# A far product weighted one tick later, and two merged first loads, in a hybrid attention and state-space trunk

## The chip, the cores and the metric

The kernel runs on one core of one Trainium2 chip. The metric is the device time of one execution in microseconds (us), the median of three runs. The core has five engines that work side by side: TensorE (PE in the profile, with its weight loads as PEld), VectorE (DVE), ScalarE (ACT), GpSimd (POOL) and SyncE (SP), and sixteen DMA engines that move data between the large memory and the core.

## The reference, cut to what matters

Two layers on 256 tokens of width 2048, each a mixer and an MLP, all in float32. Layer 0 mixes with latent attention (MLA), layer 1 with a Mamba-2 scan (SSM).

```python
def reference(x, ...):
    for i in range(DEPTH):                       # DEPTH = 2
        h = rms_norm(x, mix_norm_g[i])
        mix = mla_mixer(h, ...) if i % 2 == 0 else ssm_mixer(h, ...)
        x = x + mix
        h = rms_norm(x, mlp_norm_g[i])
        x = x + squared_relu_mlp(h, mlp_w_in[i], mlp_w_out[i])
    return x

# inside the scan of ssm_mixer, 8 groups g of 8 heads h of 64 channels p:
cb = einsum('blgn,bsgn->blsg', c_c, b_c)
y_diag = einsum('blsgh,bsghp->blghp', cb[..., None] * decay, x_c)
```

`y_diag` of the second 128 tokens gets one part from the first 128 tokens. That part is the far product: the inputs, weighted by their decay to the border of the halves, times `cb`, and then weighted by the decay from the border on.

## The kernel before, in words

**Matrix products.** Every weight is split into two rounded halves: ScalarE makes `wh` (line 102), VectorE makes `wl` = weight minus `wh` (line 103). A unit is two slices of 128 rows by 512 columns of a weight, 512 KB, loaded by SyncE into a tile `wraw` (line 85). TensorE runs over a unit 12 products of 128x512: eight with `wh` (lines 340 and 341, four of each), then four with `wl` (line 344). Loads and splits run some units ahead of TensorE; buffers of `wraw`, `wh` and `wl` come free as TensorE and the splits are done with them.

**The order of work.** TensorE's order is that of the program. Other engines get theirs from a scheduler when the kernel is built, and then run their rows strictly in that order. Side work is hung into the stream of products by `later(n, fn)`: `tick()` is called once per weight block of two units, and `fn` is run in the tick after n more ticks have passed.

**The start.** `start()` loads the first two units in two pieces of 512 columns each; after each piece, `some_x()` loads one piece of the transposed input `xT` (tiles named k). Then whole units and pieces of x alternate. `split_x` makes the halves `xt` of x on ScalarE (line 483) and VectorE (line 484). Unit 0 needs slices 0 and 1 of the first x tile, unit 1 slices 2 and 3, units 2 and 3 the second x tile.

**The SSM.** For each group g, `ahead()` lets GpSimd weight x (line 1393); two ticks later `across()` makes the far product on TensorE (line 1397) into a PSUM bank of the pool `sm` and VectorE weights it by `edge` into the tile `far` (line 1399). GpSimd adds `far` to the second half of x (line 1459) long after. The pool `sm` has two banks, handed out in program order; a product into a bank waits until all that was read from its earlier contents has been read. Other users of `sm` are the transposes of the convolution of B and C (line 1222), the products B times C (lines 1309 and 1310, read by line 1313) and the transposes of the finished output (line 323).

Of the kernel before, what the change touches and what calls it, by code (L numbers as in the profile page):

```python
# [24 lines left out]
ALU = mybir.AluOpType  # L25
# [190 lines left out]
class Trunk:  # L216
# [224 lines left out]
    def start(self, seq):  # L441
        nc, d = self.nc, self.d
        self.flow = Flow(nc, self.wp, seq, (6, 3))
        self.flow.tc = self.tc
        cst = self.c.tile([P, C_END], F32, name="cst")
        self.cst = cst
        self.ident_r = self.c.tile([P, P], F32R, name="ident")
        self.ident = self.ident_r.bitcast(F32)
        self.mhalf = self.c.tile([P, 16], F32, name="mhalf")
        warm = self.s2.tile([P, 512], F32R, tag="s2", name="warm")  # L450
        nc.vector.memset(warm.bitcast(F32), 1.0)
        bank = self.sm.tile([P, 512], F32, tag="sm", name="warmed")
        for _ in range(WARM):
            nc.tensor.matmul(bank, warm[:, :P], warm, start=True, stop=True)
        nc.gpsimd.memset(self.mhalf, -0.5)
        nc.scalar.dma_start(cst[:, C_G0:C_GQ], d["cst"][:, C_G0:C_GQ])
        nc.scalar.activation(self.stat(1), self.mhalf[:, :1], AF.Copy)
        raws = [self.ktile(self.k4, F32) for _ in range(4)]
        parts = [(0, slice(k, k + 1)) for k in range(4)] + [(1, slice(0, 2)), (1, slice(2, 4)), (2, slice(0, 4)), (3, slice(0, 4))]

        def some_x():
            j, k = parts.pop(0)
            nc.sync.dma_start(raws[j][:, k], d["xT"][j][:, k])

        self.flow.load(2, ((0, 512), (512, 1024)), some_x)
        for u in range(3, 7):
            some_x()
            self.flow.load(u)
        self.pos = self.c.tile([P, 2], I32, name="pos")
        self.x = [[self.res.tile([P, 512], F32, name=f"x{t}{n}") for n in range(4)] for t in range(2)]  # L470

        self.rs_pool = [self.c.tile([P, 4], F32, name=f"rs{i}") for i in range(2)]
        self.phase = 0
        self.xT = [(self.ktile(self.xtp), self.ktile(self.xtp)) for _ in range(4)]

        def split_x(j, ks):
            h, lo = self.xT[j]
            for k in ks:
                g = cst[:, C_G0 + 4 * j + k:C_G0 + 4 * j + k + 1]
                if (j, k) == (0, 0):  # L480
                    nc.vector.tensor_scalar(h[:, k], raws[j][:, k], g, None, ALU.mult)
                else:
                    nc.scalar.activation(h[:, k], raws[j][:, k], AF.Copy, scale=g)
                nc.vector.scalar_tensor_tensor(lo[:, k], raws[j][:, k], g, h[:, k].bitcast(F32), ALU.mult, ALU.subtract)

        split_x(0, (0,))
        self.flow.convert(1)
        split_x(0, (1, 2))
        self.flow.convert(2)
        split_x(0, (3,))  # L490
        self.flow.load(7)
        one = self.scratch()
        nc.sync.dma_start(one[:, :P], d["one"])
        nc.gpsimd.tensor_copy(self.ident_r, one[:, :P])
        nc.sync.dma_start(cst[:, C_GQ:], d["cst"][:, C_GQ:])
        nc.sync.dma_start(self.pos, d["pos"])
        split_x(1, range(4))
        ssq = self.stat(8)
        self.later(0, lambda: split_x(2, range(4)))
        self.later(1, lambda: split_x(3, range(4)))  # L500

        def stats(n):
            for t in range(2):
                nc.sync.dma_start(self.x[t][n], d["x"][t * P:(t + 1) * P, n * 512:(n + 1) * 512])
                self.square_sum(self.x[t][n], ssq[:, t * 4 + n:t * 4 + n + 1])
            if n == 3:
                self.set_rstd(ssq)

        for n, at in enumerate(X_AT):
            self.later(at, lambda n=n: stats(n))  # L510
# [666 lines left out]
    def ssm_body(self, sp, dp, gain, later):  # L1177
        nc, d, cst = self.nc, self.d, self.cst
# [8 lines left out]
        edge = sp.tile([P, 2, 64], F32, name="edge")  # L1187
# [6 lines left out]
        far = [None] * GROUPS  # L1194
# [17 lines left out]
        def behind(what):  # L1212
            return self.tc.issue_after(getattr(self.flow, what).ins)
# [108 lines left out]
        def x_rows(g, t0, n, first=3):  # L1322
            v = xD[0:P, g * 512:g * 512 + 512]
            row = v.ap[0][0]
            return bass.AP(tensor=v.tensor, offset=v.offset + (t0 * P + first) * row, ap=[[row, P], [P * row, n], [1, 512]])
# [11 lines left out]
        def x_conv(g, wait):  # L1337
            cw, tap, xts = {}, {}, []

            def weight(k):  # L1340
                cw[k] = sp.tile([P, 512], F32, tag="cw", name=f"cw{g}_{k}", bufs=3)
                nc.sync.dma_start(cw[k], d["cwx"][g][:, k * 512:(k + 1) * 512])

            def load(k):
                tap[k] = self.flow.pools["rx"].tile([P, 2, 512], F32, tag="rx", name=f"tap{g}_{k}")
                nc.sync.dma_start(tap[k], x_rows(g, 0, 2, k))

            def fetch(*todo):
                with behind("last_load"):
                    for fn in todo:  # L1350
                        fn()

            def whole():
                xts.append(xn.tile([P, 2, 512], F32, tag="xn", name=f"xtm{g}"))
                nc.sync.dma_start(xts[0], x_rows(g, 0, 2))

            both = lambda k: cw[k].unsqueeze(1).to_broadcast([P, 2, 512])
            plus = lambda v: nc.vector.tensor_tensor(xts[0], xts[0], v, ALU.add)

            def tapped(k):  # L1360
                nc.vector.tensor_tensor(tap[k], tap[k], both(k), ALU.mult)
                plus(tap[k])

            def mult():
                with behind("last_lo"):
                    nc.vector.tensor_tensor(xts[0], xts[0], both(3), ALU.mult)
                    tapped(2)
                fetch(lambda: weight(0), lambda: weight(4))

            def some():  # L1370
                with behind("last_lo"):
                    tapped(1)

            def total():
                with behind("last_lo"):
                    plus(both(4))
                    tapped(0)

            def tanh():
                tap[3] = self.flow.pools["rx"].tile([P, 2, 512], F32, tag="rx", name=f"th{g}")  # L1380
                with behind("last"):
                    nc.scalar.activation(tap[3], xts[0], AF.Tanh, scale=0.5)

            def silu():
                with behind("last_lo"):
                    nc.vector.scalar_tensor_tensor(xts[0], tap[3], 1.0, xts[0], ALU.add, ALU.mult)

            def ahead():
                x = xg[g] = [xts[0][:, t] for t in range(2)]
                heads_of = lambda v: v.rearrange("p (h f) -> p h f", h=8)  # L1390
                spread = lambda v: v[:, 8 * g:8 * g + 8].unsqueeze(2).to_broadcast([P, 8, 64])
                xw = self.scratch()
                nc.gpsimd.tensor_tensor(heads_of(xw), heads_of(x[0]), spread(edge[:, 0]), ALU.mult)

                def across():
                    b = self.bank(False)
                    nc.tensor.matmul(b, cb[g][:, P:256], xw, start=True, stop=True)
                    far[g] = sp2[0].tile([P, 512], F32, tag="far", name=f"far{g}", bufs=2)
                    nc.vector.tensor_tensor(heads_of(far[g]), heads_of(b), spread(edge[:, 1]), ALU.mult)

                self.later(2, across)

            self.later(wait, lambda: fetch(whole, lambda: weight(3), lambda: load(2), lambda: weight(2), lambda: load(1)))
            self.later(wait + 1, lambda: fetch(lambda: weight(1), lambda: load(0)))
            self.later(wait + 3, mult)
            self.later(wait + 4, some)
            self.later(wait + 4, lambda: cb_group(g))
            self.later(wait + 5, lambda: (total(), hq.extend((g, i) for i in range(8))))
            self.later(wait + 6, tanh)
            self.later(wait + 7, lambda: (silu(), ahead()))  # L1410
# [399 lines left out]
```

## Time and profile before

| | |
|---|---|
| median of 3 runs | 2279.67 us (2278.27 to 2280.44) |
| the profiled execution | 2280.21 us |
| its span, first to last instruction | 2278.4 us |
| TensorE busy | 2268.2 us, 100% |
| VectorE busy | 1967.8 us, 86% |
| ScalarE busy | 1438.9 us, 63% |
| GpSimd busy | 287.2 us, 13% |
| granted TensorE clock | 1.00 |

The time is the span and 1.8 us around it. TensorE is busy almost always, so that the places to look at are the few in which it waits.

### The profile page before, as it was taken

How to read it: one execution, taken by the hardware profiler on the slowest of the kernel's cores; microseconds unless marked ns; L12 is line 12 of the kernel's file. 1: busy time of each engine (PE TensorE's matmuls, PEld its weight loads, DVE VectorE, ACT ScalarE, POOL GpSimd, SP SyncE). 2: the span in 40 equal slices, each digit the busy share in tenths (PEclk: the TensorE clock that was granted, in tenths of full speed). 3: DMA queues.
4: the chain of work that ended last, by engine and by line, in shares of the span. 5: the costliest groups of instructions: out<-in, count | busy, mean ns of one | idle time of the engine just before them, and what ended most of it. 6: DMA issues, size and time to landing. Idle time of an engine off the chain costs nothing.

```text
span 2278.4 us, 30861 instructions
## 1 busy us (share of the span) xinstructions
PE 2268.2 (100%) x10881; PEld 1880.6 (83%) x10881; DVE 1967.8 (86%) x2257; ACT 1438.9 (63%) x2044; POOL 287.2 (13%) x339
## 2 busy tenths in 40 slices
PE   9999999999999999999999999999999999999999
PEld 7898888888888888888888788888888888888887
DVE  7786697998998898879989998976989989989995
ACT  7775475566666566566677676564665665665663
POOL 1440000000000000100002532230000000000000
PEclk9999999999999999999999999999999999999999
DMA  8545688888888887768898889877788888888874
GB/s 316 173 153 155 218 226 263 260 261 260 263 255 261 269 242 239 236 199 256 275 365 287 291 292 328 274 224 224 218 253 251 258 268 245 266 279 239 263 237 160
DMA packets 176026, 569.74 MB, mean 250 GB/s; under 512 B 20192, under 2 KB 29344, under 8 KB 175872
## 3 DMA queue, kind: packets, MB, share of 16 engines
q1 hardware_dynamic: 147808, 498.24, 65.2%
q0 software_dynamic: 16320, 56.88, 11.8%
q10 hardware_dynamic: 11744, 12.66, 1.7%
q8 instruction: 85, 1.39, 0.2%
q14 instruction: 69, 0.57, 0.1%
HBM read 542.23 MB, written 6.41 MB: 241 GB/s over the span
## 4 chain that ended last, share of the span: by engine, by line
PE 96%; DVE 2%; DMA 1%; ACT 1%; issue 0%; POOL 0%; SPq 0%; ACTq 0%; DVEq 0%
PE acc L340 10%; PE acc L341 10%; PE acc L344 10%; PE yp L621 9%; PE yp L619 9%; PE yp L620 9%; PE st L620 8%; PE st L621 8%; PE st L619 8%; PE st L1164 1%; PE st L1163 1%; PE st L1162 1%; PE yp L341 1%; PE yp L340 1%; PE yp L344 1%; PE sm L325 1%
## 5 line engine op out<-in xcount | busy, mean ns | idle before, releaser
L102 ACT ACTIVATE wh<-wraw 128x1024 fp32r<-128x1024 f32 (+1 forms) x818 | 853.9, 1053 | 524.6 <-PE acc L341 188.2
L103 DVE TENSOR_TENSOR wl<-wraw,wh 128x1024 fp32r<-128x1024 f32 (+1 forms) x818 | 986.3, 1225 | 175.6 <-ACT wh L102 167.0
L619 PE MATMUL yp<-wh,k 128*128 128x512 f32 x896 | 349.3, 390 | 0.0
L621 PE MATMUL yp<-wh,k 128*128 128x512 f32 x896 | 348.8, 389 | 0.0
L620 PE MATMUL yp<-wl,k 128*128 128x512 f32 x896 | 348.6, 389 | 0.0
L102 ACT ACTIVATE wh<-wrx 128x1024 fp32r<-128x1024 f32 x192 | 202.8, 1059 | 171.9 <-PE yp L621 98.2
L103 DVE TENSOR_TENSOR wl<-wrx,wh 128x1024 fp32r<-128x1024 f32 x192 | 233.7, 1221 | 51.6 <-ACT wh L102 49.7
L621 PEld LDWEIGHTS yp<-wh,k 128*128 128x128 f32 x896 | 168.1, 188 | 35.1
L619 PEld LDWEIGHTS yp<-wh,k 128*128 128x128 f32 x896 | 168.2, 188 | 34.9
L620 PEld LDWEIGHTS yp<-wl,k 128*128 128x128 f32 x896 | 168.2, 188 | 34.8
L340 PE MATMUL acc<-wh,k 128*128 128x512 f32 x496 | 196.4, 396 | 0.0
L341 PE MATMUL acc<-wh,k 128*128 128x512 f32 x496 | 193.4, 390 | 0.0
L340 PE MATMUL acc<-wh,xt 128*128 128x512 f32 x480 | 192.2, 400 | 0.4 <-ACT wh L102 0.4
L341 PE MATMUL acc<-wh,xt 128*128 128x512 f32 x480 | 187.8, 391 | 0.0
L619 PE MATMUL st<-wh,xt 128*128 128x512 f32 x448 | 177.7, 397 | 0.0
L621 PE MATMUL st<-wh,xt 128*128 128x512 f32 x448 | 174.9, 390 | 0.0
L620 PE MATMUL st<-wl,xt 128*128 128x512 f32 x448 | 174.7, 390 | 0.0
L200 POOL DMA_DIRECT2D wrx<-mi x56 | 49.1, 877 | 740.8 <-DVE wl L103 550.1
L620 PE MATMUL st<-wl,sN 128*128 128x512 f32 x336 | 131.5, 391 | 2.6 <-DVE wl L103 2.6
L619 PE MATMUL st<-wh,sN 128*128 128x512 f32 x336 | 133.1, 396 | 0.0
L344 PE MATMUL acc<-wl,k 128*128 128x512 f32 x496 | 132.7, 389 | 0.0
L621 PE MATMUL st<-wh,sN 128*128 128x512 f32 x336 | 131.2, 390 | 0.0
(342 smaller groups left out, 3814.0 us busy)
## 6 DMA issues: line engine op xcount, KB each, us to landing
wraw<-mi SPq DMA_DIRECT2D x256, 512.0 KB, 5.6
wraw<-mo SPq DMA_DIRECT2D x256, 512.0 KB, 5.4
wraw<-si SPq DMA_DIRECT2D x160, 512.0 KB, 6.0
wraw<-so SPq DMA_DIRECT2D x64, 512.0 KB, 4.9
wrx<-mi SPq DMA_DIRECT2D x56, 512.0 KB, 5.4
wrx<-mi POOLq DMA_DIRECT2D x56, 512.0 KB, 7.8
wraw<-wo SPq DMA_DIRECT2D x32, 512.0 KB, 3.9
tap<-xD SPq DMA_DIRECT2D x24, 512.0 KB, 8.0
```

Source lines behind the costliest of these rows:

```text
L102: self.last = nc.scalar.activation(h[:, v], raw[:, v], AF.Copy)
L103: self.last_lo = nc.vector.tensor_tensor(lo[:, v], raw[:, v], h[:, v].bitcast(F32), ALU.subtract)
L200: nc.gpsimd.dma_start(st["b11"].tile, quarter(d, 1, 0), accum_op=ALU.add)
L325: self.nc.tensor.transpose(b[:, v], src[:, v], self.ident)
L340: nc.tensor.matmul(accs[t][:, :n], ah, wh[:, q, :], start=first and kt + q == 0, stop=False)
L341: nc.tensor.matmul(accs[t][:, :n], al, wh[:, q, :], start=False, stop=False)
L344: nc.tensor.matmul(accs[t][:, :n], lhs(kt + q, t)[0], wl[:, q, :], start=False, stop=en and q == nk - 1)
L619: nc.tensor.matmul(b, ah, wh, start=first and q == 0, stop=False)
L620: nc.tensor.matmul(b, ah, wl, start=False, stop=False)
L621: nc.tensor.matmul(b, al, wh, start=False, stop=last and q == 1)
L1162: nc.tensor.matmul(bank[onto], ah, wh, start=done + q == 0 and not skip, stop=False, skip_group_check=skip)
L1163: nc.tensor.matmul(bank[onto], al, wh, start=False, stop=False, skip_group_check=skip)
```

## The change

Two edits. In the SSM, the VectorE weighting of the far product moves out of `across()` into a function that is called one tick later. In the start, unit 0 is still loaded in two pieces, each followed by one slice of x; then slices 2 and 3 of x come as one transfer of 256 KB (two of 128 KB before), then unit 1 as one transfer of 512 KB (two of 256 KB before), and from there on all goes as it did.

```diff
-        parts = [(0, slice(k, k + 1)) for k in range(4)] + [(1, slice(0, 2)), (1, slice(2, 4)), (2, slice(0, 4)), (3, slice(0, 4))]
+        parts = [(0, slice(0, 1)), (0, slice(1, 2)), (0, slice(2, 4)), (1, slice(0, 2)), (1, slice(2, 4)), (2, slice(0, 4)), (3, slice(0, 4))]
...
-        self.flow.load(2, ((0, 512), (512, 1024)), some_x)
+        self.flow.load(1, ((0, 512), (512, 1024)), some_x)
+        some_x()
+        self.flow.load(2)
...
-                    nc.vector.tensor_tensor(heads_of(far[g]), heads_of(b), spread(edge[:, 1]), ALU.mult)
+
+                    def weigh():
+                        nc.vector.tensor_tensor(heads_of(far[g]), heads_of(b), spread(edge[:, 1]), ALU.mult)
+
+                    self.later(0, weigh)
```

TensorE's own order stays row for row what it was. The order of the other engines changes at the start and in the SSM. Numbers at the end of a name only count tiles.

SyncE's queue at the start of the program, before (wraw_119 is unit 0, wraw_124 unit 1, wraw_130 unit 2; k_2 is the first x tile, k_3 the second):

```order
L85 DMA wraw_119<-ain 128x512
L463 DMA k_2_115<-xT 128x256
L85 DMA wraw_119<-ain 128x512
L463 DMA k_2_115<-xT 128x256
L85 DMA wraw_124<-ain 128x512
L463 DMA k_2_115<-xT 128x256
L85 DMA wraw_124<-ain 128x512
L463 DMA k_2_115<-xT 128x256
L463 DMA k_3_116<-xT 128x512
L85 DMA wraw_130<-ain 128x1024
```

The same place of the change (wraw_125 is unit 1, wraw_128 unit 2):

```order
L85 DMA wraw_119<-ain 128x512
L463 DMA k_2_115<-xT 128x256
L85 DMA wraw_119<-ain 128x512
L463 DMA k_2_115<-xT 128x256
L463 DMA k_2_115<-xT 128x512
L85 DMA wraw_125<-ain 128x1024
L463 DMA k_3_116<-xT 128x512
L85 DMA wraw_128<-ain 128x1024
```

Unit 2 now stands behind seven transfers instead of nine, which carry the same bytes.

VectorE around the weighting of group 0's far product, before (xtm and tap are the convolution of x, cb the products B times C; sm_806 is the bank of the far product):

```order
L1358 TENSOR_TENSOR xtm1_10885<-xtm1_10885,tap1_2_10889 128x1024
L1399 TENSOR_TENSOR far0_11078<-sm_806_11076,edge_8831 128x512
L103 TENSOR_TENSOR wl543_11095<-wraw543_10987,wh543_11094 128x1024
L103 TENSOR_TENSOR wl544_11113<-wraw544_11033,wh544_11112 128x1024
L1361 TENSOR_TENSOR tap1_1_10893<-tap1_1_10893,cw1_1_10951 128x1024
L1313 SCALAR_TENSOR_TENSOR cb1_11133<-sm_808_11130,tri_8827 128x128
```

The same place of the change, where the weighting is line 1403:

```order
L1360 TENSOR_TENSOR xtm1_10883<-xtm1_10883,tap1_2_10887 128x1024
L103 TENSOR_TENSOR wl543_11092<-wraw543_10985,wh543_11091 128x1024
L103 TENSOR_TENSOR wl544_11110<-wraw544_11031,wh544_11109 128x1024
L1363 TENSOR_TENSOR tap1_1_10891<-tap1_1_10891,cw1_1_10949 128x1024
L1403 TENSOR_TENSOR far0_11076<-sm_806_11074,edge_8829 128x512
L1360 TENSOR_TENSOR xtm1_10883<-xtm1_10883,tap1_1_10891 128x1024
```

And TensorE of the change, a tick behind the far product, with the waits: sm_808 is in the pool's other bank, and sm_809, the transposes of line 1224 (1222 before), in the bank that sm_806 had, so that its wait for VectorE is the wait for that weighting, before as after:

```order
L1311 MATMUL sm_808_11127<-k4_743_9294,k4_717_9010 128x256 [waits Activation_49]
L1312 MATMUL sm_808_11127<-k4_743_9294,k4_717_9010 128x128
L1224 MATMUL sm_809_11133<-ident_97,s2_798_10907 128x128 [waits DVE_49,PE_49]
L1224 MATMUL sm_809_11133<-ident_97,s2_799_10909 128x128
L1224 MATMUL sm_809_11133<-ident_97,s2_798_10907 128x128
```

The weighting moved behind two splits and a tap product, with the same reader of its bank behind it. In the other groups the next product into the bank of the far product stands at least 51 TensorE rows behind it, here 27.

VectorE around the weighting of group 1's far product, before (mt12 are decays of heads, wl557 the half of a weight):

```order
L1399 TENSOR_TENSOR far1_11570<-sm_843_11568,edge_8831 128x512
L1440 TENSOR_TENSOR mt12_11515<-mt12_11515,cb1_11133 128x512 x2
L103 TENSOR_TENSOR wl557_11587<-wraw557_11470,wh557_11586 128x1024
L103 TENSOR_TENSOR wl558_11605<-wraw558_11524,wh558_11604 128x1024
L1358 TENSOR_TENSOR xtm2_11300<-xtm2_11300,cw2_4_11493 128x1024
L1361 TENSOR_TENSOR tap2_0_11355<-tap2_0_11355,cw2_0_11491 128x1024
```

The same place of the change:

```order
L1446 TENSOR_TENSOR mt12_11513<-mt12_11513,cb1_11130 128x512 x2
L103 TENSOR_TENSOR wl557_11584<-wraw557_11468,wh557_11583 128x1024
L103 TENSOR_TENSOR wl558_11602<-wraw558_11522,wh558_11601 128x1024
L1360 TENSOR_TENSOR xtm2_11298<-xtm2_11298,cw2_4_11491 128x1024
L1363 TENSOR_TENSOR tap2_0_11353<-tap2_0_11353,cw2_0_11489 128x1024
L1403 TENSOR_TENSOR far1_11568<-sm_843_11566,edge_8829 128x512
```

Here the weighting no longer stands ahead of wl557. In groups 2, 5 and 6 it moves by one to four rows; in groups 3, 4 and 7 VectorE's order stays as it was. Some ScalarE rows of the SSM (exponentials of heads and weight splits) change places with their neighbours, and so do two small loads with unit loads on SyncE.

## Rows read from the trace of the kernel before

**Rows 1.** The page: busy time of each engine, and the chain that ended last.

```profile
PE 2268.2 (100%) x10881; PEld 1880.6 (83%) x10881; DVE 1967.8 (86%) x2257; ACT 1438.9 (63%) x2044; POOL 287.2 (13%) x339
...
PE 96%; DVE 2%; DMA 1%; ACT 1%; issue 0%; POOL 0%; SPq 0%; ACTq 0%; DVEq 0%
```

**Rows 2.** Waits of TensorE, whole span: total us, times, longest us.

```profile
PE acc L344 <- DVE wl L103: 1.5, 1, 1.5
...
PE acc L340 <- ACT wh L102: 0.4, 1, 0.4
```

**Rows 3.** Timeline of the start, TensorE, then ScalarE: start us, duration us, work.

```profile
9.26 0.39 PE L340 MATMUL acc<-wh,xt 128*128 128x512 f32 x1
...
11.20 1.08 PE L344 MATMUL acc<-wl,xt 128*128 128x512 f32 x4
12.65 0.50 PE L340 MATMUL acc<-wh,xt 128*128 128x512 f32 x1 [0.37 <-ACT wh L102]
...
8.59 0.63 ACT L102 ACTIVATE wh<-wraw 128x512 fp32r<-128x512 f32 x1 [0.46 <-DMA wraw<-ain]
...
11.54 1.06 ACT L102 ACTIVATE wh<-wraw 128x1024 fp32r<-128x1024 f32 x1 [0.87 <-DMA wraw<-ain]
```

**Rows 4.** SyncE's issues of x slice 3 and unit 2, and their us to landing.

```profile
4.38 0.80 SPq L463 DMA_DIRECT2D k<-xT  x2
5.22 0.43 SPq L85 DMA_DIRECT2D wraw<-ain  x1
...
k<-xT SPq DMA_DIRECT2D x1, 128.0 KB, 4.7
...
wraw<-ain SPq DMA_DIRECT2D x1, 512.0 KB, 6.3
```

**Rows 5.** Two stretches of the start; last columns: clock, DMA busy share, GB/s.

```profile
6.00:8.00 2.00, 2.00 (x7) 1.61 (x7) 1.35 (x4) 1.23 (x3) 0.00 (x0) 1.00 0.94 305
...
12.00:14.00 2.00, 1.63 (x8) 1.13 (x7) 1.37 (x2) 1.91 (x4) 0.00 (x0) 1.00 1.02 418
```

**Rows 6.** Timeline around group 0's weighting, VectorE, then TensorE.

```profile
1208.10 0.69 DVE L1399 TENSOR_TENSOR far<-sm,edge 128x512 f32<-128x512 f32 x1
1208.70 2.35 DVE L103 TENSOR_TENSOR wl<-wraw,wh 128x1024 fp32r<-128x1024 f32 x2
1210.97 1.22 DVE L1361 TENSOR_TENSOR tap<-tap,cw 128x1024 f32<-128x1024 f32 x1
1212.11 0.28 DVE L1313 SCALAR_TENSOR_TENSOR cb<-sm,tri 128x128 f32<-128x128 f32 x1
...
1204.31 1.02 PE L1397 MATMUL sm<-s,cb 128*128 128x512 f32 x2
...
1211.31 0.60 PE L1222 MATMUL sm<-ident,s 128*128 128x128 f32 x4
```

**Rows 7.** Timeline around group 1's weighting, VectorE, then TensorE.

```profile
1257.69 0.68 DVE L1399 TENSOR_TENSOR far<-sm,edge 128x512 f32<-128x512 f32 x1
1258.29 1.29 DVE L1440 TENSOR_TENSOR mt<-mt,cb 128x512 f32<-128x512 f32 x2
1259.49 2.36 DVE L103 TENSOR_TENSOR wl<-wraw,wh 128x1024 fp32r<-128x1024 f32 x2
...
1258.90 0.39 PE L341 MATMUL acc<-wh,xt 128*128 128x512 f32 x1
1260.77 1.20 PE L344 MATMUL acc<-wl,xt 128*128 128x512 f32 x4 [1.48 <-DVE wl L103]
```

**Rows 8.** Between the two: a wait of VectorE and one of ScalarE; GpSimd's use of far.

```profile
DVE wl L103 <- ACT wh L102: 0.9, 1, 0.9
...
1221.75 1.06 ACT L102 ACTIVATE wh<-wraw 128x1024 fp32r<-128x1024 f32 x1 [0.48 <-PE acc L341]
...
1228.12 1.36 POOL L1459 TENSOR_TENSOR xtm<-xtm,far 128x512 f32<-128x512 f32 x1
...
1274.50 1.62 POOL L1459 TENSOR_TENSOR xtm<-xtm,far 128x512 f32<-128x512 f32 x1
```

## The prediction, made before the changed kernel was run

> **What bounds the kernel now.** I first read the page. TensorE is busy 2268.2 of 2278.4 us, and the chain that ended last is TensorE for 96% [rows 1]. Only 10.2 us of the span are left in which it does nothing, so 10.2 us is about all that an edit of waits can win, and what TensorE has to compute stays the same here. What I look for is therefore every place where TensorE waits and that the edits touch, and every place where the edits make a new wait. The view of waits of TensorE names, among a few, two that are near the edits [rows 2]: 1.5 us, once, of line 344 for a weight half of VectorE, and 0.4 us, once, of line 340 for a weight half of ScalarE. The timelines show where they are. The second is at 12.65 us, the first product of unit 2 [rows 3]; the first is at 1260.77 us, in the SSM, right after VectorE has weighted group 1's far product [rows 7]. All else in the SSM keeps up with TensorE.
>
> **The start.** Unit 2's wait ends with a transfer: ScalarE sat idle for unit 2's load until 11.54 and split for 1.06 us, and TensorE began at 12.65 [rows 3]. The load was issued at 5.22 and took 6.3 us to land, so it landed at 11.52 [rows 4], 1.13 us ahead of TensorE's start. TensorE could have begun earlier: the last four products of unit 1 begin at 11.20, one product takes 0.23 us of the engine in a full stream (eight from 9.26 on and four behind them bring it from 9.26 to about 12.11), so it lost 12.65 - 12.11 = 0.54 us. That is the most the start can win.
>
> How much earlier does unit 2 land? The issue is not the limit: it left the queue 6.3 us before it landed, while SyncE spends some 0.45 us on an issue [rows 4]. The transfer engines are: from 6 to 8 us they are busy 0.94 of the time, at 305 GB/s, while later, with whole units alone, they are busy 1.02 and move 418 GB/s [rows 5]. The bytes ahead of unit 2 stay the same, so what can change is this rate. Unit 1 and x slices 2 and 3 are 768 KB, 786 thousand bytes: 2.58 us at 305, 1.88 us at 418. If the merged transfers all ran at the rate of whole units, unit 2 would land 0.70 us earlier; if size made no difference, not at all. The x slices only reach half the size of a unit, and part of the low rate may be the first filling of the engines, so I take half, 0.35 us. The ends are 0 and 0.54 (where TensorE's own work becomes the limit).
>
> Merging has a price: the first half of unit 1 was at hand early, and now nothing of unit 1 is until all of it has landed. At worst that is when the same bytes had landed before, with x slice 3, at 4.38 + 4.7 = 9.08 us [rows 4]. ScalarE then needs 0.63 us for the first half of its split [rows 3], so TensorE would begin unit 1 at about 9.77 in place of 9.26, and reach unit 2 at 12.62. That still is before 12.65, so the price is hidden under the wait for unit 2: the landing of unit 2 decides, and unit 1 can cost nothing on top. Without that cover it would be 0.51 us. The units behind are split from loads that come earlier by the same amount. **Term: -0.35 us**, between -0.54 and 0.
>
> **Group 0's far product.** TensorE makes it at 1204.31 and wants the same bank back for the convolution's transposes at 1211.31, one tick later; VectorE read the bank from 1208.10 and was done 2.4 us before that [rows 6]. In the change, two weight halves and a tap product stand ahead of the weighting. These three took VectorE from 1208.70 to 1212.11, 3.41 us, without a gap [rows 6]; their inputs were there. So the weighting begins at 1208.10 + 3.41 = 1211.51 and ends 0.69 us later, at 1212.20. From the end of a VectorE row to the TensorE row that waited for it I count 0.06 us: at the second place the first of two halves from 1259.49 ends at about 1260.71 and TensorE goes on at 1260.77 [rows 7]. The transposes begin at 1212.26 and not 1211.31. TensorE runs its rows in order, so all products behind them wait too. **Term: +0.95 us**, from 0.85 to 1.15 (the weight load of the first transpose may come on top).
>
> Is it given back? VectorE's backlog at the second place would have to be independent of TensorE. It is not: between the two places VectorE waited 0.9 us for a weight half of ScalarE, and ScalarE for TensorE [rows 8], which releases the buffers of halves. A TensorE that is 0.95 us late makes these late too. I take it as kept.
>
> Here a rule speaks against the change. The Trainium skill, "PSUM — Partial Sum Buffer", section "Summary: rules for kernel authors", says to empty PSUM promptly, since it is small. By that rule alone, holding the bank a tick longer should cost in all eight groups. The rows and the order say where it does: only where the bank is asked back a tick later. That is group 0, with 27 TensorE rows between; in the others at least 51 lie between, over 11 us at 0.23 us each, and VectorE's order moves by a few rows.
>
> **Group 1's far product.** Here VectorE is late. The weighting starts at 1257.69, the decays of heads at 1258.29, the weight half that TensorE waits for at 1259.49 [rows 7]. In the change the weighting no longer stands ahead of it, which brings the half forward by 1258.29 - 1257.69 = 0.60 us. TensorE waits 1.48 us there, so all of 0.60 is won. The weighting itself now comes some 6 us later, behind the decays, the two halves and two products of the convolution; GpSimd takes its result only at 1274.50, and for group 0 at 1228.12 [rows 8], so both have ten us and more to spare. **Term: -0.60 us**, to -1.48 if VectorE has gained elsewhere too.
>
> **The rest at nothing.** Two weight splits and some exponentials of ScalarE, and two small loads on SyncE, change places with a neighbour; TensorE waits for none of them in the rows, and a shift of one row is about 1 us. GpSimd's order is the same. Groups 2, 5 and 6 move a weighting of 0.69 us on a VectorE that TensorE doesn't wait for there. If that cover were gone, each costs at most its 0.6 us.
>
> **Sum.** -0.35 + 0.95 - 0.60 = 0.00 us. The profiled execution, 2280.21, would stay at 2280.2. It lies 0.54 us above the median of the runs shown, so the forecast for the median is 2279.7 us. A change of under 0.2% (4.6 us) is about what a measurement of this kernel can't tell from none.
>
> **The rivals.**
> *The stall of group 0 is paid back at group 1.* VectorE would have its work done while TensorE waits, and the 1.48 us at 1260.77 would vanish whole: -0.35 + 0.95 - 1.48 = -0.88, 2278.8 us. For it: VectorE is without a gap for most of that stretch. Against it: its wait of 0.9 us in between. Chance 0.15.
> *The start wins nothing.* The rate of the transfers is that of a start, not of their size: +0.95 - 0.60 = +0.35, 2280.0 us. For it: x slice 3, a quarter of unit 2's bytes, takes 4.7 us to land, not much less than unit 2's 6.3 [rows 4]. Chance 0.15.
> *The bank is not missed.* If VectorE were ahead of its rows of before by 1 us at 1208, the later weighting would cost nothing, and the change would not do what it does in my sum: -0.95, 2278.7 us. Against it: nothing ahead of it on VectorE is changed. Chance 0.05.
> *The bank is missed everywhere,* the rule's case and the one on the other side: the stall of 0.95 us in eight groups is 7.6, and 7.6 - 0.60 - 0.35 = +6.65, 2286.3 us. It decides from some five groups on. It needs VectorE to be over 4 us behind where 51 and more TensorE rows lie between. Chance 0.04.
> *Faster than 0.2%* needs 4.6 of the 10.2 us of idle TensorE, most of which the edits don't touch. Chance 0.02.
>
> **How the numbers follow.** The forecast has 0.59. The range reaches from below the two cases at 2278.7 to above the case at 2280.0 and the upper bounds of the terms (0 + 1.15 - 0.60 = +0.55, 2280.2), widened on both sides by the 0.8 to 1.4 us by which single runs of before lie off their median: 2278.0 to 2281.2. Within 0.2% are the first four cases, 0.94; slower 0.04; faster 0.02.
>
> **What would show it.** In the changed kernel's profile, unit 2's first product should begin near 12.3, with ScalarE's split of it near 11.2. The transposes of line 1224 near 1212 should show a wait of about 0.9 us for VectorE's weighting, which should stand behind line 1363. The wait of line 344 for a weight half near 1260 should be about 0.9 us and not 1.48. No other wait of TensorE over 0.5 us should be new in the SSM. The prediction is wrong if the transposes start without a wait, if the wait at 1260 stays or goes whole, if unit 2 lands at 11.5 or later, or if a wait appears in another group.

## The result, and the profile after

The changed kernel takes 2285.04 us (median of 18 runs, 2283.38 to 2288.49), the kernel before 2280.49 us in the same sessions (18 runs). The ratio is 1.0023, with a 95% interval of 1.0015 to 1.003: slower by about 5 us, and outside the range that was forecast.

The page of the changed kernel, busy time and share of the chain, which answer to [rows 1]:

```profile
PE 2270.7 (99%) x10881; PEld 1882.1 (82%) x10881; DVE 1971.6 (86%) x2257; ACT 1437.8 (63%) x2044; POOL 271.0 (12%) x339
...
PE 95%; DVE 2%; DMA 1%; ACT 1%; issue 0%; POOL 0%; SPq 0%; DVEq 0%; ACTq 0%
```

GpSimd's recorded time fell from 287.2 to 271.0 us with the same 339 instructions, and VectorE's rose by 3.8 us. Both will matter. Its view of TensorE's waits (total us, times, longest us), beside [rows 2]:

```profile
PE acc L341 <- DVE k L301: 1.7, 1, 1.7
...
PE sm L1224 <- DVE far L1403: 1.4, 1, 1.4
PE acc L344 <- DVE wl L103: 1.3, 1, 1.3
...
PE acc L340 <- ACT k L300: 1.0, 1, 1.0
```

The wait at L1224 was forecast, the wait at L344 was forecast to shrink. The two on `k` stand nowhere in the prediction. `k` is the transposed output of two groups, split by ScalarE (line 300) and VectorE (line 301), with which the output projection starts.

To see where the time goes I cut TensorE's timeline at rows that stand in both kernels: the far product of group 0, and the first product of `y` (the decays times x) of groups 0, 1, 2 and 3. Before (start us, duration us, work; the other cuts are at 1204.31, [rows 6], and 1299.15):

```profile
1217.31 2.08 PE L1453 MATMUL y<-xtm,mt 128*64 128x64 f32 x64
1261.89 2.08 PE L1453 MATMUL y<-xtm,mt 128*64 128x64 f32 x64
1341.94 2.09 PE L1453 MATMUL y<-xtm,mt 128*64 128x64 f32 x64
```

After:

```profile
1202.20 1.02 PE L1399 MATMUL sm<-s,cb 128*128 128x512 f32 x2
1216.77 2.08 PE L1459 MATMUL y<-xtm,mt 128*64 128x64 f32 x64
1261.21 2.08 PE L1459 MATMUL y<-xtm,mt 128*64 128x64 f32 x64
1298.74 2.08 PE L1459 MATMUL y<-xtm,mt 128*64 128x64 f32 x64
1346.28 2.08 PE L1459 MATMUL y<-xtm,mt 128*64 128x64 f32 x64
```

| stage of TensorE | before, us | after, us | difference |
|---|---|---|---|
| A: far product of group 0 to y of group 0 | 13.00 | 14.57 | +1.57 |
| B: to y of group 1 | 44.58 | 44.44 | -0.14 |
| C: to y of group 2 | 37.26 | 37.53 | +0.27 |
| D: to y of group 3 | 42.79 | 47.54 | +4.75 |

From there to TensorE's last product the changed kernel loses another 0.4 us. So most of the loss is stage D, in which the two waits on `k` lie, and stage A holds another 1.57 us. The 2.1 us by which the changed kernel is ahead at group 0 are not the edit's: the kernel with the far edit and the old start, below, is there at 1202.32. The profile of before had two waits, of 0.74 us near 571 and 0.54 us near 738, in code that the edit doesn't touch, which the profile of the changed kernel has not.

**What happens in D.** VectorE and GpSimd around 1300 us, first of before (`x2` is two rows told as one; brackets have the engine's wait ahead of the row and what ended it):

```profile
1299.73 0.28 DVE L1313 SCALAR_TENSOR_TENSOR cb<-sm,tri 128x128 f32<-128x128 f32 x1
1299.93 2.35 DVE L103 TENSOR_TENSOR wl<-wraw,wh 128x1024 fp32r<-128x1024 f32 x2
1302.20 1.21 DVE L1358 TENSOR_TENSOR xtm<-xtm,cw 128x1024 f32<-128x1024 f32 x1
...
1301.27 9.09 POOL L1457 TENSOR_TENSOR xtm<-xtm,gb 128x512 f32<-128x512 f32 x2 [12.97 <-issue]
```

and of the changed kernel:

```profile
1300.62 0.68 DVE L1403 TENSOR_TENSOR far<-sm,edge 128x512 f32<-128x512 f32 x1
1301.22 4.26 DVE L103 TENSOR_TENSOR wl<-wraw,wh 128x1024 fp32r<-128x1024 f32 x2
1305.40 2.31 DVE L1360 TENSOR_TENSOR xtm<-xtm,cw 128x1024 f32<-128x1024 f32 x1
...
1300.86 3.54 POOL L1463 TENSOR_TENSOR xtm<-xtm,gb 128x512 f32<-128x512 f32 x2 [11.27 <-issue]
```

GpSimd multiplies x by the gain `dg` as soon as TensorE has finished `y`. Before, that moment falls under a split of VectorE, which reads two tiles in SBUF, and GpSimd needs 9.09 us for its two rows. After, it falls under the weighting, which reads PSUM, and GpSimd needs 3.54 us; but now VectorE's next two splits take 4.26 us instead of 2.35 and the row behind them 2.31 instead of 1.21, 3.0 us lost. Those 3.0 us go down a chain: the sum of the convolution on VectorE, then `tanh` on ScalarE, and all that is queued behind it. ScalarE in the changed kernel:

```profile
1311.15 1.07 ACT L1384 ACTIVATE th<-xtm 128x1024 f32<-128x1024 f32 x1 [5.43 <-DVE xtm L1360]
...
1318.46 1.06 ACT L300 ACTIVATE k<-sm 128x512 fp32r<-128x512 f32 x2
```

(before: `tanh` at 1306.85 after a wait of 1.81, line 300 at 1314.17). The 4.30 us by which `tanh` is later are these 3.0, 0.6 for the weighting that now stands ahead, and 0.7 by which VectorE was late at 1300 already (below). Then come VectorE's halves of `k` (line 301 at 1320.56, 1317.74 before), and TensorE:

```profile
1317.69 0.39 PE L344 MATMUL acc<-wl,k 128*128 128x512 f32 x1
1319.09 0.49 PE L340 MATMUL acc<-wh,k 128*128 128x512 f32 x1 [1.01 <-ACT k L300]
1321.30 0.50 PE L341 MATMUL acc<-wh,k 128*128 128x512 f32 x1 [1.71 <-DVE k L301]
```

Two steps that take 0.23 us each in a full stream take 1.40 and 2.21 us, so 3.15 us are lost by waiting. Before, VectorE made its two halves one behind the other, of 0.68 us each, and TensorE needed them at 1318.56 and 1319.07:

```profile
1317.74 1.28 DVE L301 TENSOR_TENSOR k<-sm,k 128x512 fp32r<-128x512 f32 x2
...
1318.56 0.41 PE L341 MATMUL acc<-wh,k 128*128 128x512 f32 x1
...
1319.07 0.50 PE L341 MATMUL acc<-wh,k 128*128 128x512 f32 x1
```

That is 0.14 us behind the first half and 0.05 us behind the second: there was hardly any slack. What is left of the 4.75 us is in these stretches (us, TensorE busy and its products, granted clock, DMA share, GB/s):

```profile
1316.00:1321.30 5.30, 2.58 (x12) 1.00 0.76 224
1321.30:1325.00 3.70, 3.70 (x9) 0.56 1.04 395
```

After the wait the granted clock is 0.56 on average over 3.70 us, mostly at the lower of its two levels (1.2 of 2.4 GHz), which costs 3.70 x 0.44 = 1.6 us. 3.15 + 1.63 = 4.78 is all but the 4.75.

Why is VectorE later at this place, when TensorE is 0.4 us earlier? It had met GpSimd once already, in stage B. VectorE and GpSimd of the changed kernel there, where the weighting is that of group 1 and the products of GpSimd are group 1's:

```profile
1263.36 0.68 DVE L1403 TENSOR_TENSOR far<-sm,edge 128x512 f32<-128x512 f32 x1
1263.96 1.75 DVE L1360 TENSOR_TENSOR xtm<-xtm,tap 128x1024 f32<-128x1024 f32 x1
1265.63 4.55 DVE L103 TENSOR_TENSOR wl<-wraw,wh 128x1024 fp32r<-128x1024 f32 x2
...
1263.34 3.53 POOL L1463 TENSOR_TENSOR xtm<-xtm,gb 128x512 f32<-128x512 f32 x2 [5.54 <-issue]
```

Before, GpSimd began at 1264.01 under a split and needed 10.41 us for the two. Here VectorE loses 0.53 us in line 1360 (1.22 before) and 2.19 in the two splits (2.36 before), 2.7 in all. The kernel before pays more when GpSimd at last comes through (four rows from 1273.8 to 1282 are 3.6 us longer than usual, 2.1 in the changed kernel), so that 1.2 us of VectorE's lateness against TensorE remain. They are seen at 1300: line 1315 stands at 1299.73 before and at 1300.42 in the changed kernel, 0.7 us later, while TensorE is 0.4 us earlier. That brings the rows which read PSUM under GpSimd's release.

### The profile page after: what moved, and what is told of

It is laid out like the page before. It is cut to its first block, busy times and chain, and to the rows that moved or that the text cites. A ratio compares the mean times of both kernels' runs of the same rounds, so it can differ in the third digit from the quotient of the medians.

```text
span 2283.3 us, 30863 instructions
## 1 busy us (share of the span) xinstructions
PE 2270.7 (99%) x10881; PEld 1882.1 (82%) x10881; DVE 1971.6 (86%) x2257; ACT 1437.8 (63%) x2044; POOL 271.0 (12%) x339
## 4 chain that ended last, share of the span: by engine, by line
PE 95%; DVE 2%; DMA 1%; ACT 1%; issue 0%; POOL 0%; SPq 0%; DVEq 0%; ACTq 0%
PE acc L340 10%; PE acc L341 10%; PE acc L344 10%; PE yp L623 10%; PE yp L621 10%; PE yp L622 10%; PE st L622 8%; PE st L623 8%; PE st L621 8%; PE st L1166 1%; PE st L1165 1%; PE st L1164 1%; PE yp L341 1%; PE yp L340 1%; PE yp L344 1%; DVE wl L103 1%
## 5 line engine op out<-in xcount | busy, mean ns | idle before, releaser
L344 PE MATMUL acc<-wl,k 128*128 128x512 f32 x496 | 133.2, 390 | 0.0
```

The costliest lines, as they stand in the source:

```text
L344: nc.tensor.matmul(accs[t][:, :n], lhs(kt + q, t)[0], wl[:, q, :], start=False, stop=en and q == nk - 1)
```

## The experiments

All take the changed kernel as their base unless their edit says otherwise; `weigh()` at once is the old place. The table has the result of each beside the readings of its profile: ratio to the kernel before with its interval, TensorE's stages A, B and D as above, and GpSimd's two products of groups 1 and 2 (near 1262 and 1300).

| kernel | ratio (95%) | A | B | D | GpSimd, us |
|---|---|---|---|---|---|
| before | | 13.00 | 44.58 | 42.79 | 10.4, 9.1 |
| changed | 1.0023 (1.0015 to 1.003) | 14.57 | 44.44 | 47.54 | 3.5, 3.5 |
| start only | 1.0000 (0.9991 to 1.0008) | 13.00 | 44.50 | 42.78 | 10.4, 9.1 |
| far only | 1.0022 (1.0013 to 1.0031) | 13.89 | 43.61 | 47.79 | 3.5, 3.7 |
| all but group 2 | 1.0026 (1.0015 to 1.0036) | 14.69 | 44.27 | 47.80 | 3.5, 3.7 |
| group 2 only | 1.0002 (0.9993 to 1.0011) | 13.00 | 44.87 | 42.77 | 10.4, 9.1 |
| group 1 only | 1.0018 (1.0009 to 1.0027) | 13.00 | 44.19 | 46.07 | 3.5, 3.6 |
| all but group 1 | 1.0005 (0.9996 to 1.0014) | 14.27 | 44.24 | 42.77 | 10.4, 9.1 |
| twice, PSUM | 1.0014 (1.0005 to 1.0022) | 13.00 | 44.58 | 47.50 | 3.5, 3.5 |
| maximum, SBUF | 1.0003 (0.9995 to 1.0012) | 13.00 | 45.33 | 43.37 | 11.0, 9.7 |
| all but 0 and 1 | 0.9999 (0.9990 to 1.0008) | 13.00 | 44.40 | 42.77 | 10.4, 9.1 |
| group 1, copied | 1.0002 (0.9993 to 1.0011) | 13.00 | 43.83 | 43.38 | 11.0, 9.7 |
| no GpSimd, group 0 | 1.0020 (1.0011 to 1.0029) | 14.05 | 42.86 | 48.65 | 3.5, 3.5 |
| no GpSimd, group 1 | 0.9999 (0.9990 to 1.0008) | 14.31 | 44.35 | 43.64 | none, 9.9 |

In every kernel a GpSimd pair of some 3.5 us near 1300 goes with a long D, and one of 9 us or more with a short one.

**Start only.**

```diff
-                    self.later(0, weigh)
+                    weigh()
```

Expected:

> The new first loads alone; every far product is weighted at its old place. Three theories of the 4.6 us that the change lost. MEETING: the loss is made in one place, at group 2, where the later weighting (which reads PSUM) runs just when GpSimd's products of the group before are released, so that GpSimd's work and VectorE's splits slow each other; then this kernel has none of it: the kernel before less the 0.33 us measured at the start, about 0.35 us faster (ratio 0.9998), products x*dg of group 1 on GpSimd near 9 us for two at 1301, no wait of TensorE over 0.5 us between 1290 and 1340. SUM OF DELAYS: each of the eight weightings pushes VectorE back by 0.6 us and these add up until TensorE waits; the same 0.35 us faster here. START: the new first loads shift the stream of weights and are themselves the cause; then 4 to 5 us slower here.

Measured: 2280.08 us against 2279.89, ratio 1.0000. The loss is not the start's; its gain isn't to be seen either.

**Far only,** with the lines of `start()` as before:

```diff
...
-        self.flow.load(1, ((0, 512), (512, 1024)), some_x)
-        some_x()
-        self.flow.load(2)
+        self.flow.load(2, ((0, 512), (512, 1024)), some_x)
```

Expected:

> The later weighting alone in all eight groups, with the old first loads. MEETING and SUM OF DELAYS: the whole loss and none of the start's gain, 4.9 to 5.3 us slower than before (ratio 1.002), waits at the output projection's first products on k near 1319 to 1322 as in the changed kernel. START: within 1.5 us of the kernel before.

Measured: 1.0022, both waits on `k` (1.2 and 1.7 us). START falls.

**All but group 2** and **group 2 only.**

```diff
-                    self.later(0, weigh)
+                    if g in (0, 1, 3, 4, 5, 6, 7,):
+                        self.later(0, weigh)
+                    else:
+                        weigh()
```

Expected of the first:

> The changed kernel with group 2's far product weighted at its old place, the other seven a tick later. MEETING: the 4.75 us at group 2 go; what stays is -0.33 at the start, +1.4 at group 0 (wait of the row shifts L1224 for the weighting), -0.1 at group 1: 1.0 us slower than before (ratio 1.0004), no wait over 0.5 us on k near 1320, GpSimd's two products x*dg of group 1 near 9 us instead of 3.5. SUM OF DELAYS: only one delay of 0.6 us less, so 3.5 to 4 us slower than before, with a wait of 2 us or more left near 1320.

Measured: 1.0026, D as long as in the changed kernel. MEETING in the form that I gave it is wrong: it doesn't need group 2's weighting. SUM OF DELAYS, which wanted most of the loss to stay, is not yet excluded. The rows of VectorE and GpSimd say what took the weighting's place:

```profile
1300.42 1.22 DVE L1360 TENSOR_TENSOR xtm<-xtm,tap 128x1024 f32<-128x1024 f32 x1
1301.56 0.29 DVE L1315 SCALAR_TENSOR_TENSOR cb<-sm,tri 128x128 f32<-128x128 f32 x1
1301.76 4.35 DVE L103 TENSOR_TENSOR wl<-wraw,wh 128x1024 fp32r<-128x1024 f32 x2
...
1301.34 3.69 POOL L1466 TENSOR_TENSOR xtm<-xtm,gb 128x512 f32<-128x512 f32 x2 [11.21 <-issue]
```

Another row that reads PSUM, line 1315, now stands at the moment, because VectorE is late. Before, it had ended at 1300.01, 1.26 us ahead of GpSimd's start.

The second has `if g in (2,):` in the same place. Expected:

> The new first loads, and the later weighting in group 2 alone. MEETING: it depends on the moment, which the trace will show. VectorE comes to the place 0.7 us earlier than in the changed kernel (the delays of groups 0 and 1 are gone), so the weighting should run from about 1299.6 to 1300.3, and GpSimd's products are released at about 1300.9: if the weighting is over by then, GpSimd stays shut out (about 9 us for its two products), VectorE is late by 0.6 us alone, and the time is 0 to 0.6 us over that of the kernel with the start alone; if they meet, 3.5 us for GpSimd's two, 4.3 for VectorE's two splits, and 4 to 5 us slower. SUM OF DELAYS: 0 to 0.6 us over the start alone, whatever GpSimd does. START: as the start alone.

Measured: 1.0002, GpSimd shut out, D unchanged. Group 2's own later weighting is harmless, so something earlier makes VectorE late.

**Group 1 only** (`if g in (1,):`) and **all but group 1** (`if g in (0, 2, 3, 4, 5, 6, 7,):`). Their expectations call the products near 1262 those of group 0; the numbers in the names of the tiles show that they are group 1's own, which changes nothing in the argument.

Expected of the first:

> The new first loads, and the later weighting in group 1 alone. The meeting at group 2 survived there without group 2's own later weighting, so the theory is now ROOT AT GROUP 1: group 1's later weighting reads PSUM and runs just when GpSimd's products of group 0 are released (near 1262); GpSimd gets in, VectorE's next splits are slowed, VectorE arrives late at group 2's place, where another operation that reads PSUM lets GpSimd in again, and TensorE waits near 1320. Then this kernel alone shows the whole of it: 4 to 5 us over the kernel with the start alone (about 2284.5), GpSimd's two products 3.5 us instead of 10.4 near 1262 and 3.5 to 3.7 instead of 9.1 near 1300, and the waits of 1.0 and 1.7 us on k. SUM OF DELAYS (each later weighting only pushes VectorE by 0.6 us, in all groups alike): 0 to 0.6 us over the start alone.

Measured: 1.0018, with the waits of 1.07 and 1.71 us on `k`. One weighting out of eight makes the loss. D is 3.3 us longer than in the start alone, and not 4.75, for in the profiled execution the clock stayed up after the wait:

```profile
1316.00:1320.30 4.30, 1.53 (x7) 1.00 0.81 236
1320.30:1324.00 3.70, 3.70 (x16) 1.00 1.03 388
```

So the wait alone is worth 3.2 us, and the clock comes on top where it falls: of the 11 executions, the five with a mean granted clock of 0.998 took 2284.3 to 2286.9 us, and the two at 1.000 took 2282.1 and 2282.9.

Expected of the second:

> The changed kernel with group 1's far product weighted at its old place, the other seven a tick later. ROOT AT GROUP 1: the 4.75 us near 1320 are gone, GpSimd's products take 10.4 and 9.1 us again; what stays is the start's -0.33 and group 0's wait of 1.4 us, so 0.5 to 1.5 us over the kernel before (2280.4 to 2281.4). SUM OF DELAYS: nearly all of the loss stays, 3.5 us or more over the kernel before.

Measured: 1.0005, no wait on `k`; A is 1.27 us longer, by the wait of L1224 alone (1.1 us). Both directions agree: ROOT AT GROUP 1 holds, SUM OF DELAYS falls.

**Twice, PSUM** and **maximum, SBUF.** A pair that differs in what one VectorE row of group 1 reads. The first:

```diff
-                    self.later(0, weigh)
+                    weigh()
+                    if g == 1:
+                        self.later(0, weigh)
```

Expected:

> The kernel with the new first loads alone, and in group 1 the weighting done twice: at its old place, and again from the same PSUM bank where the changed kernel has it (0.68 us of VectorE more; the same values are written again). WHAT IT READS MATTERS: the second weighting reads PSUM when GpSimd is released, so GpSimd gets in: two products in 3.5 us near 1262, VectorE's splits behind it 4.5 instead of 2.35 us for two, and 4 to 6 us over the kernel with the start alone. ONLY THE DELAY MATTERS: 0.7 us more of VectorE, the same in this kernel and in its twin that works in SBUF.

The second has, as its last line:

```diff
+                        self.later(0, lambda: nc.vector.tensor_tensor(far[g], far[g], far[g], ALU.max))
```

Expected:

> The twin of the kernel that weighs twice: at the second place VectorE takes the maximum of the finished far product with itself, so the same 128x512 numbers, but two inputs in SBUF and none in PSUM. Order and count of VectorE's instructions are the same. WHAT IT READS MATTERS: GpSimd stays shut out near 1262 (10 us or more for its two products), VectorE is late by 0.7 us alone, and the time is 0 to 0.7 us over the kernel with the start alone, 4 us under its twin. ONLY THE DELAY MATTERS: the same time as its twin, within 0.5 us.

Measured: 1.0014 and 1.0003, 2282.89 and 2280.38 us in the same session. VectorE and GpSimd of the first:

```profile
1262.94 0.68 DVE L1403 TENSOR_TENSOR far<-sm,edge 128x512 f32<-128x512 f32 x1
1263.54 1.75 DVE L1360 TENSOR_TENSOR xtm<-xtm,tap 128x1024 f32<-128x1024 f32 x1
1265.21 4.55 DVE L103 TENSOR_TENSOR wl<-wraw,wh 128x1024 fp32r<-128x1024 f32 x2
...
1262.92 3.53 POOL L1465 TENSOR_TENSOR xtm<-xtm,gb 128x512 f32<-128x512 f32 x2 [6.14 <-issue]
```

and of the second:

```profile
1263.79 0.68 DVE L1407 TENSOR_TENSOR far<-far 128x512 f32<-128x512 f32 x1
1264.39 1.21 DVE L1360 TENSOR_TENSOR xtm<-xtm,tap 128x1024 f32<-128x1024 f32 x1
1265.53 2.35 DVE L103 TENSOR_TENSOR wl<-wraw,wh 128x1024 fp32r<-128x1024 f32 x2
...
1263.77 11.00 POOL L1465 TENSOR_TENSOR xtm<-xtm,gb 128x512 f32<-128x512 f32 x2 [6.13 <-issue]
```

The same 0.68 us at the same place lets GpSimd in when it reads PSUM, and keeps it out when it reads SBUF twice. ONLY THE DELAY MATTERS falls. By the medians the pair is 2.5 us apart where I expected 4, and the two intervals overlap, so it is the rows above that decide; in the profiles D differs by 4.1, and B by 0.75 the other way, since the second waited 2.2 us at L344.

**All but groups 0 and 1** (`if g in (2, 3, 4, 5, 6, 7,):`). Expected:

> The changed kernel with groups 0 and 1 weighted at their old places, groups 2 to 7 a tick later. If groups 0 and 1 hold all of the loss, this is the kernel with the start alone, within 0.6 us (ratio 0.9998 to 1.0003): no wait on far, none on k over 0.5 us, and against the kernel without group 1 alone the wait of 1.1 us at the row shifts L1224 is gone. If the six other weightings cost 0.6 us each on the path, 2 us or more over the kernel with the start alone.

Measured: 0.9999, A, B and D as before. Six of the eight later weightings cost nothing; in three of the six (groups 3, 4 and 7) VectorE's order is the same either way.

**Group 1, copied.**

```diff
-                    self.later(0, weigh)
+                    if g == 1:
+                        nc.scalar.activation(far[g], b, AF.Copy)
+                        self.later(0, lambda: nc.vector.tensor_tensor(heads_of(far[g]), heads_of(far[g]), spread(edge[:, 1]), ALU.mult))
+                    else:
+                        weigh()
```

Expected:

> The new first loads, and group 1's far product weighted a tick later as in the change, but from SBUF: ScalarE first copies it out of PSUM (0.7 us of ScalarE), and VectorE then multiplies two inputs that are both in SBUF. VectorE's row has the same order and the same count as in the kernel where group 1 alone is later. WHAT IT READS MATTERS: GpSimd's two products stay at 10 us near 1262, the waits on k are gone, and the time is 3 to 5 us under the kernel where group 1 alone is later, about that of the start alone or, since the weighting no longer stands ahead of the two splits that TensorE waits for near 1259, up to 0.6 us under it. ONLY THE DELAY MATTERS: as the kernel where group 1 alone is later.

Measured: 1.0002, GpSimd shut out (11.0 us), and the wait at L344 down to 0.73 us with B at 43.83. This keeps the gain that the change was forecast to have at group 1 and avoids the meeting. D pays 0.6 us of it back, and no measured gain over the kernel before is left.

**No GpSimd in group 0** and **in group 1.**

```diff
                     x = xg[g][t]
+                    if g == 0:
+                        continue
                     nc.gpsimd.tensor_tensor(x, x, dg, ALU.mult)
```

Expected of the first:

> The changed kernel without GpSimd's three operations of group 0 (its two products x*dg and the addition of far are left out, so group 0's share of the result lacks them). IT TAKES TWO: with nothing for GpSimd to do near 1263 the later weighting of group 1 costs VectorE 0.6 us at most, its two splits behind it take 2.35 us instead of 4.55, VectorE comes to group 2's place in time, the waits on k go, and the time is that of the kernel without group 1's later weighting or some tenths less, 2279.5 to 2281. THE WEIGHTING ALONE: with or without GpSimd the later place costs the same, and the time stays at 2284 to 2285.

Measured: 1.0020. The operations near 1262 were still there, as group 0's stand at 1219: this kernel leaves out the wrong ones, and tells only that those of group 0 are no part of it.

The second has `if g == 1:`. Expected:

> The run before this one left out the wrong operations: those of group 0 stand at 1219, and the ones near 1262 are group 1's own (its two products x*dg and the addition of its far product), as the tiles' numbers in the rows show. Here it is these three that GpSimd leaves out, so group 1's share of the result lacks them; all else is the changed kernel. IT TAKES TWO: with nothing for GpSimd to do near 1262 the later weighting of group 1 costs VectorE 0.6 us at most, its two splits behind it take 2.35 us instead of 4.55, VectorE comes to group 2's place in time, GpSimd is shut out there (9 us or more for its two products near 1300), the waits on k go, and the time is about that of the kernel without group 1's later weighting, 2279.5 to 2281.5. THE WEIGHTING ALONE: with or without GpSimd the later place costs the same, and the time stays at 2284 to 2285.

Measured: 0.9999. VectorE at both places:

```profile
1264.45 0.69 DVE L1403 TENSOR_TENSOR far<-sm,edge 128x512 f32<-128x512 f32 x1
1265.05 1.22 DVE L1360 TENSOR_TENSOR xtm<-xtm,tap 128x1024 f32<-128x1024 f32 x1
1266.18 2.36 DVE L103 TENSOR_TENSOR wl<-wraw,wh 128x1024 fp32r<-128x1024 f32 x2
...
1300.61 0.68 DVE L1403 TENSOR_TENSOR far<-sm,edge 128x512 f32<-128x512 f32 x1
1301.21 2.35 DVE L103 TENSOR_TENSOR wl<-wraw,wh 128x1024 fp32r<-128x1024 f32 x2
```

Order and VectorE's work are those of the changed kernel. Without GpSimd's three rows near 1262 nothing is lengthened there, and the second meeting, 37 us later, does not come about: GpSimd starts at 1301.71, 0.42 us after the weighting has ended, and is shut out. D is still 0.9 us longer than before, with a wait of 0.6 us for `k`: VectorE's own lateness costs that much where hardly any slack is. No kernel here has the second meeting without the first, so its 3.0 us are read from rows and not isolated.

No version beats the kernel before by more than the measurement can tell.

## Why the prediction was wrong, step by step

**The step that failed** is in "Group 1's far product". It costed the move by who reads `far` ("both have ten us and more to spare") and by who waits for VectorE's half. It did not ask what the moved row would stand beside. A row of VectorE that reads PSUM was put on the moment at which GpSimd is released, and that let GpSimd's three rows in between VectorE's: GpSimd's two products took 3.5 us instead of 10.4, VectorE lost 2.7 us there and 3.0 us at the second meeting, and stage D grew by 4.75 us, for which the prediction had nothing. Group 1's move alone makes both waits on `k`, 3.3 us of D in a profile whose clock stayed up, and the change without it has neither.

**"The rest at nothing"** failed with it. The cover that was named, a VectorE that TensorE doesn't wait for in groups 2, 5 and 6, was right for the moved rows themselves: moving them cost nothing. But the ceiling "at most its 0.6 us" leaves out that VectorE's rows can get longer, and that 0.14 and 0.05 us were left at the output projection. Rows 1 and 2 list where TensorE's products wait, and "all else in the SSM keeps up" was read from them. The near miss stands in the list of its weight loads, of the kernel before:

```profile
PEld acc L341 <- DVE k L301: 0.5, 2, 0.3
```

**Group 0, +0.95.** The mechanism is right, with the wait at L1224 for the weighting behind line 1363, as forecast, and only in the kernels in which group 0 is late. The size was a little low: in the six such profiles A is 13.89 to 14.69 us, 0.9 to 1.7 over the 13.00 of all the others, 1.3 on the mean.

**Group 1, -0.60.** The seven kernels with a later weighting there have B at 43.9 us on the mean (42.86 to 44.44), the five with it at the old place alone 44.5 (44.24 to 44.87). So about -0.6 was right as a mean of B, but the changed kernel's profile, at -0.14, shows little of it: single profiles differ by more than the term. Nor is it kept: over B and C together the seven take 81.6 us on the mean and the five 81.8, and with the far edit alone C is 38.76 us, by a wait of 1.0 us for a weight half.

**The start, -0.35.** Unit 2's first product came at 12.48 in the changed kernel instead of 12.65 [rows 3], without a wait. But with the old start and the far edit it came at 12.34, and in the last kernel above, with the new start, at 13.48. The step that failed here is "unit 1 can cost nothing on top": it was counted as hidden under the wait for unit 2. In the kernel with the new start alone TensorE waits for unit 1 instead, and unit 2 follows without a wait, at 12.64:

```profile
9.79 0.50 PE L340 MATMUL acc<-wh,xt 128*128 128x512 f32 x1 [0.63 <-ACT wh L102]
```

In the twelve profiles with the new start unit 1 begins at 9.24 to 10.63, 9.9 on the mean (9.26 and 9.32 with the old one; the worst that was forecast is 9.77), and unit 2 at 12.10 to 13.48, 12.8 on the mean. The start alone is at ratio 1.0000. The rival "the start wins nothing" has the number that the runs support, but what they show is a wait that moved from unit 2 to unit 1.

**The rival on the other side** had nearly the right number, 2286.3 us, for the wrong reason: a bank missed in all eight groups. The bank is missed in group 0 alone. The reason given against it was sound. And 4.6 us is not "what a measurement of this kernel can't tell from none": the change lost 4.55 us by the medians, and the interval excludes a ratio of 1.

The Trainium skill bears on the step that failed: "SBUF — State Buffer", section "Who interferes with whom", says that a VectorE instruction with two inputs in SBUF contends with a GpSimd instruction that reads SBUF. Section "SBUF: two separate sides" of the same page of the Trainium skill says that whichever of the two starts first holds the shared pair of ports for the whole instruction, while the other is blocked. The pair of kernels above agrees: 3.53 us for GpSimd's two rows where VectorE read PSUM, 11.00 where it read SBUF twice. It is a rule that I should have weighed, since GpSimd's 9 and 10 us for two rows stood in the trace of before.

## What to carry to other kernels

Before a VectorE row is moved, look at what GpSimd is released to do at the new place, and at whether the row reads PSUM: in these traces a chain of VectorE rows with two SBUF inputs kept GpSimd out without getting longer itself, and one row with a PSUM input in it opened the door. An engine that is slow without hurting anyone (GpSimd at 9 us for two rows of 1.3) may be slow to the benefit of another. And a list of the waits of TensorE's products doesn't show near misses; the list for its weight loads showed this one. For each transfer of work between engines ahead of TensorE, also read the distance from the end of the last row to the product that needs it.

## What the runs showed of the hardware

The two products of GpSimd at 1301 in the kernel before, by line (shortest, median and longest in ns):

```profile
L1457 POOL TENSOR_TENSOR xtm<-xtm,gb x2: 1287/4562/7837, 1301.3 to 1309.1; 128x512 f32<-128x512 f32 x2
```

GpSimd's multiplication of 128x512 takes 1.29 us where nothing is in its way, and took 7.84 us against VectorE rows with two SBUF inputs, one behind the other: GpSimd did not get its turn at the end of a VectorE row, only when VectorE read PSUM (at 1267.4 and 1273.2 in the kernel before) or stood still (at 1307.9). Once GpSimd had got in near 1301 in the changed kernel, the rows read as if the two took turns: VectorE's two splits of 1.21 us took 2.02 and 2.32 us, and GpSimd's second product 2.28. By the Trainium skill's section "SBUF: two separate sides" named above the other would be blocked until the first instruction finishes; here GpSimd stayed blocked over six of them, and the measurement decides. Why the turns alternate in the one case and not in the other, no run here shows.

After the same wait on `k` TensorE's granted clock was 1.00 throughout in one profile (group 1 only) and fell to 0.50 in the others with that wait: for some 3 us in the changed kernel, and over the whole of a stretch of 6 us (1320 to 1326) in the kernel without GpSimd's group 0. What decides it stays open; it is 1.6 us of the 4.75 in the changed kernel.
